# A hybrid decoder layer on one core: which engine adds the second product's weight parts, when its first finished rows are written, and how the first product's raw weights are loaded

## Chip, cores and metric

The kernel runs on one core of a Trainium2 chip. The metric is the device time of one execution in microseconds (us); lower is better. Before the change it took 2276.67 us, the median of three runs (2275.1, 2276.67 and 2277.1). Line numbers L... are those of the kernel before.

## What is computed

One decoder layer over 2048 tokens of width 1024, in float32: a block of gated linear attention and dilated attention, and behind it an MLP with a squared ReLU. The change touches the MLP alone:

```python
nm = rmsnorm(h, mlp_norm_g[l])
a = jnp.square(jax.nn.relu(jnp.einsum('bsd,df->bsf', nm, w_ff1[l])))
h = h + jnp.einsum('bsf,fd->bsd', a, w_ff2[l])
...
return rmsnorm(h, final_norm_g)
```

w_ff1 is 1024 x 4096 and w_ff2 is 4096 x 1024.

## The kernel before

**Precision.** Every float32 operand of a matmul is split in two parts: `hi`, a rounded copy made by ScalarE, and `lo`, the rest, made by VectorE (`split`, L485 to L487). A product is then three matmuls (`mm3`, L141 to L144): hi by hi, lo by hi, hi by lo. The rows "L486 ACT" and "L487 DVE" of the profile are these splits, whatever is split. In `mm3` the second matmul (L143) is the first that needs the stationary operand's `lo`.

**First product (nm by w_ff1).** It uses Winograd's form of Strassen's scheme: a 2 x 2 block product in 7 products instead of 8. The outer loop runs over 32 groups g: two halves of the tokens, and in each 16 blocks of 256 columns of w_ff1. Each group has seven products j in the order 1, 2, 6, 5, 7, 3, 4, of 12 matmuls each. The raw weights of a group (1 MB) are loaded into one of two buffers `raw1` by `load_w1` (L1282 to L1287, tile `w1raw`); `prep1` (L1289 to L1309) makes the sums of weight blocks that the scheme needs, in place (L1302, L1303, L1305, L1307, VectorE), and splits the block that product j takes into one of four buffers `w1comb`. `prep1` runs two products ahead of `product1`. When the last product's block (j = 4) is split, the buffer is free, and the load of group g + 2 is issued. `product1` takes the results out of PSUM: L1371 and L1385 on ScalarE, L1373, L1377 and L1381 on VectorE. Products 1, 6, 7 and 4 of a group add up in one PSUM bank, 5 and 3 in another; so product 4 cannot start before L1377 has read what stands after product 7. Where the second half of the tokens begins, 14 pieces of the transposed activations are loaded (tile `rb<-hTD`, L1596) and split (tile `hb`) beside the products. Sums of the results (L1335, VectorE) go to DRAM in `actD`, for the second product.

**Second product (act by w_ff2).** It has 26 phases, one for each line of the table `PRODUCTS`: a scheme of 4 x 4 by 4 x 2 blocks. A line lists which parts of w_ff2 make up the right operand and which output blocks take the result. The weights are built up step by step in a state (`state_of`, tile `bs`) of four slots, one for each quarter of a phase; a quarter is counted as n = 4 * phase + k. A part with "=" is loaded over the slot (L1497); a part with "+" or "-" is loaded into one of four buffers (`fetch_b`, L1476 to L1488, tile `rb<-w_ff`) and added or subtracted by `update_b` (L1490 to L1499). A slot can be updated for n + 4 only when the splits of n have read it. Three phases (5, 7 and 8) add two parts, sixteen add one; the first phase's updates name their own engines (V, V), which the change leaves alone. `prep_b` splits the state (tile `cb`), `prep_a` the left operand (tile `ca`, L486/L487, or L1458/L1459 where the product counts negative), both into three buffers in turn. Each n then has 24 matmuls. Within a phase the loop issues `update_b(n + 4)`, `fetch_b(n + 6)`, `prep_a(n + 2)`, `prep_b(n + 2)`, the PSUM sums of the phase before (`taken`, L1551 to L1565: L1557 on ScalarE where a block begins, L1560 on VectorE else), and the matmuls.

**Finished rows.** `done_at` holds, for each row block k of the output, the last phase that adds to it: 24, 23, 20 and 25 for k = 0 to 3. When it is taken, `output` (L1510 to L1527) normalizes four row tiles (ScalarE for the squares and the root, VectorE L1521 and L1525) and stores them. Residual rows are added into the output blocks by accumulating DMAs from GpSimd's queue (L1548).

**What sets the order.** The attention's instructions stand in a hand-written order. From the output projection on, the program is handed to a scheduler, which orders each engine's instructions by a model of their times; the Python order is its input. Each engine then runs its own list in order: an instruction that waits holds up all behind it on that engine.

Of the kernel before, what the change touches and what calls it, by code (L numbers as in the profile page):

```python
# [14 lines left out]
OP = mybir.AluOpType  # L15
# [95 lines left out]
NPH = len(PRODUCTS)  # L111
# [5 lines left out]
def emit(tc, a, stop=99):  # L117
    nc = tc.nc
    V, A, G, T, SP = nc.vector, nc.scalar, nc.gpsimd, nc.tensor, nc.sync
# [9 lines left out]
    def slot(name, dt=F32, n=SLOT):  # L129

        return up.tile([128, SLOT], dt, name=name, tag="u", bufs=25)[:, :n]

    def view(t, shape):
        n = int(np.prod(shape))
        names = "abcd"[:len(shape)]
        return t[:, :n].rearrange(f"p ({' '.join(names)}) -> p {' '.join(names)}", **dict(zip(names, shape)))
# [252 lines left out]
    def taken(n, t):  # L389

        i = t % 4
        A.activation(outputs(0)[2 * n + t // 4][:, 256 * i:256 * i + 512], held["first", n, t], AF.Copy)
        for m in (i, i + 1):
            finish(0, n, t // 4, m)
# [90 lines left out]
    def split(hi, lo, src):  # L485
        A.activation(hi, src, AF.Copy)  # L486
        V.tensor_tensor(lo, src, hi.bitcast(F32), op=OP.subtract)  # L487
# [124 lines left out]
    with tc.manual_schedule(engines={nc.tensor.engine, nc.vector.engine, nc.scalar.engine, nc.gpsimd.engine}):  # L612
# [59 lines left out]
        pv = turned(3)  # L672
        block(1, 1, 0)
        taken(0, 0)
        x_scale(4)
        first_half(3, pv)
# [9 lines left out]
        x_stat(6)  # L686
        first_half(4, pv)
        taken(1, 0)
        pv = turned(5)
        both(0, 3)  # L690
# [4 lines left out]
        both(0, 4)  # L695
        x_scale(7)
        taken(0, 2)
        first_half(6, pv)
        pv = turned(7)
# [32 lines left out]
    for at in range(7, len(jobs)):  # L732
        g = jobs[at][0]
# [542 lines left out]
    w1 = a["w_ff1"].rearrange("o (c p) n -> p (o c) n", p=128)  # L1276
# [2 lines left out]
    jobs1 = [(g, j) for g in range(2 * NP) for j in order]  # L1279
    raw1, combs1, acc1 = [], [], []  # L1280

    def load_w1(g):  # L1282
        if g < 2 * NP:
            if len(raw1) < 2:
                raw1.append(view(slot("w1raw"), (CH, 256)))
            g0 = g % NP * 256
            SP.dma_start(raw1[g % 2], w1[:, :, g0:g0 + 256])  # L1287

    def prep1(at):  # L1289

        if at >= len(jobs1):
            return
        g, j = jobs1[at]
        if not combs1:
            combs1.extend(view(c[:, 1024 * q:], (2, 4, 128)) for c in [slot("w1comb", FR) for _ in range(2)]
                          for q in range(2))
        r = raw1[g % 2]
        (a11, a12), (a21, a22) = [[r[:, 4 * k:4 * k + 4, n * 128:n * 128 + 128] for k in range(2)] for n in range(2)]
        c = combs1[at % 4]
        split(c[:, 0], c[:, 1], {1: a11, 2: a12, 6: a11, 5: a21, 7: a11, 3: a12, 4: a22}[j])  # L1300
        if j == 1:
            V.tensor_tensor(a21, a21, a22, op=OP.add)  # L1302
            V.tensor_tensor(a11, a21, a11, op=OP.subtract)  # L1303
        if j == 2:
            V.tensor_tensor(a12, a12, a11, op=OP.subtract)  # L1305
        if j == 6:
            V.tensor_tensor(a11, a22, a11, op=OP.subtract)  # L1307
        if j == 4:
            load_w1(g + 2)  # L1309

    tags = list("acdcadco")

# [87 lines left out]
    for at, t in enumerate(tiles):  # L1400
# [24 lines left out]
        if at == W1AT:  # L1425
            load_w1(0)
        if at == W1AT + 1:
            prep1(0)
            prep1(1)
# [33 lines left out]
    fetched = {}  # L1463

    def w2_part(n, k, m):

        first = 8 * (n % 4) + 2 * (k % 2) + k // 2
        return w2[:, first:first + 5:4, 512 * m:512 * m + 512]

    def state_of(n):  # L1470

        if len(state) < 2:
            state.extend(view(slot("bs"), (4, 512)) for _ in range(2))
        return state[n % 4 // 2][:, n % 2 * 2:n % 2 * 2 + 2]
# [12 lines left out]
                SP.dma_start(v, w2_part(n, k, m))  # L1487
                fetched[n].append((op, v))  # L1488

    def update_b(n, engines=(G, V)):  # L1490

        if n >= LAST:
            return
        v = state_of(n)
        for op, k, m in PRODUCTS[n // 4][2]:
            if op == "=":
                SP.dma_start(v, w2_part(n, k, m))  # L1497
        for e, (op, r) in enumerate(fetched.pop(n)):
            engines[e].tensor_tensor(v, v, r, op=OP.add if op == "+" else OP.subtract)  # L1499

    def prep_b(n):

# [7 lines left out]
    def output(C, row, i, last=False):  # L1510

        scr = fin["scr"][:, 512 * (i % 2):512 * (i % 2) + 512]
        ss, part = stat(2), stat()
        for n in range(2):
            A.activation(scr, C[n], AF.Square, accum_out=ss[:, n:n + 1])
            if n == 0:
                if last:
                    G.tensor_tensor(C[0], C[0], fin["g"][:, :512], op=OP.mult)
                A.activation(part, ss[:, 0:1], AF.Copy, bias=EPS, scale=1.0 / D)
        r = rstd_of(ss[:, 1:2], D, bias=part)  # L1520
        V.scalar_tensor_tensor(C[1], C[1], r, fin["g"][:, 512:], op0=OP.mult, op1=OP.mult)  # L1521
        if last:
            A.activation(C[0], C[0], AF.Copy, scale=r)
        else:
            V.scalar_tensor_tensor(C[0], C[0], r, fin["g"][:, :512], op0=OP.mult, op1=OP.mult)  # L1525
        SP.dma_start(out2[row:row + 128, 512:], C[1])
        (A if last else SP).dma_start(out2[row:row + 128, :512], C[0])  # L1527
# [23 lines left out]
    def taken(ph, i, p):  # L1551

        for op, k, m in PRODUCTS[ph][3]:
            if began[k, m] == ph:
                if i == 0:
                    acc2[k, m] = view(slot("sum"), (4, 512))
                A.activation(acc2[k, m][:, i], p, AF.Copy, scale=1.0 if op == "+" else -1.0)  # L1557
                continue
            v = acc2[k, m][:, i]
            V.tensor_tensor(v, v, p, op=OP.add if op == "+" else OP.subtract)  # L1560
        for k, n in done_at.items():
            if n == ph:
                half, m = divmod(i, 2)
                output([acc2[k, n][:, i] for n in range(2)], 1024 * half + 256 * k + 128 * m, i,
                       ph == NPH - 1 and i == 3)  # L1565
# [7 lines left out]
    rb.append(slot("rb"))  # L1573
    back = [*back, reload(order[3], 0), reload(order[4], 0), reload(order[5], 0, slot("rt"))]
    load_w1(1)
    for at in range(7):
        if at == 2:
            norm_to_T(*late)
        if back:
            list(back.pop(0))  # L1580
        if at == 1:
            back.append(reload(order[6], 0))
        prep1(at + 2)
        some_sums()
        product1(at)
# [12 lines left out]
    for at in range(7, len(jobs1)):  # L1598
        if at == first - 3:
            for n in range(4):  # L1600
                load_piece(n)
        prep1(at + 2)
        some_sums()
        product1(at)
        for n in parts_at.get(at, ()):
            cs = slice(1024 * (n % 2), 1024 * (n % 2) + 1024)
            split(*[v[:, cs] for v in TF[order[n // 2]]], piece(n))
            load_piece(n + 4)
        n = at + 6 - len(jobs1)
        if n == 0:  # L1610
            load_a(0)
        if 0 <= n < 4:
            fetch_b(n)
            update_b(n, (V, V))
        if n == 3:
            load_a(1)
        if n in (3, 5):
            prep_b(n // 2 - 1)
            prep_a(n // 2 - 1)
            fetch_b(n // 2 + 3)  # L1620
# [4 lines left out]
    for ph, (_, chained, _, _) in enumerate(PRODUCTS):  # L1625
        if not chained:
            held2[ph % 2] = [ps(t) for t in ("acdc", "adco")[ph % 2]]
        P = held2[ph % 2]
        for k in range(4):
            n = 4 * ph + k  # L1630
            update_b(n + 4)
            if n + 6 not in fetched:
                fetch_b(n + 6)
            prep_a(n + 2)
            prep_b(n + 2)
            if k == 1:
                begin(ph)
            if left:
                taken(ph - 1, k, left[k])
            if ph < NPH - 1 or k < 2:  # L1640
                for c in range(2):
                    for i in range(4):
                        mm2(P[i], n, c, i, not chained)
        left = P
# [60 lines left out]
```

## Time and profile before

| what | value |
|---|---|
| median of three runs | 2276.67 us |
| the profiled execution | 2279.83 us, of which the span from first to last instruction is 2278.1 us |
| granted TensorE clock, mean | 0.997 |
| first product | about 1076 to 1699 us of the span |
| second product | about 1686 to 2269.5 us of the span, overlapping the first at its start |
| behind the last matmul | 8.5 us, for the last row tile's norm and stores |

A row of the timeline gives start, duration, engine, line, operation, output<-inputs, shape and type, and in brackets how long the engine sat idle before it and what ended that. A row of the table by stage gives the stretch, its length, then busy us and number of instructions (x) of TensorE's matmuls, its weight loads, VectorE, ScalarE and GpSimd, and at the end the granted clock, the mean share of time in which the core's DMA engines were busy, and GB/s. A row of groups gives busy us and mean ns of one behind the first bar, idle time before them behind the second. A row of waits gives us in total, times and the longest. A row of DMA issues gives their number, KB each, and median us from issue to landing.

In the names of engines PE is TensorE, PEld its weight loads, DVE is VectorE, ACT is ScalarE, POOL is GpSimd and SP is SyncE (SPq: its queue of DMA issues).

### The profile page before, as it was taken

The page shows a single profiled execution, that of the slowest core. Times are in us where ns is not written, and L with a number is a line of the kernel's source. Part 1 is how long each engine was busy: PE and PEld are TensorE (multiplying, and loading weights), DVE is VectorE, ACT ScalarE, POOL GpSimd, SP SyncE. Part 2 cuts the span into 40 slices and gives each one's busy share as a digit, 9 for nine tenths or more (in the row PEclk, how much of TensorE's full clock was granted, in tenths as well). Part 3 has the DMA queues.
Part 4 walks back from the last instruction along what each step waited for, and adds up shares of the span by engine and source line. Part 5 has one row for each costly group of instructions (what it writes and reads, how often), then busy time and mean ns, then how long its engine had stood idle before and what let it go on. Part 6 is the DMA issues. An engine that isn't in the chain of part 4 may idle for free.

```text
span 2278.1 us, 35114 instructions
## 1 busy us (share of the span) xinstructions
PE 2245.7 (99%) x12508; PEld 1941.4 (85%) x12508; DVE 1627.7 (71%) x3080; ACT 1221.2 (54%) x2421; POOL 520.0 (23%) x467
## 2 busy tenths in 40 slices
PE   9999999999999999999999999999999999999998
PEld 8978998899999998888788887888888878888876
DVE  8787878766667676445777778767685567566788
ACT  6665446426877883324555557555555433333435
POOL 1210002024385673000000000000006563042452
PEclk9999999999999999999999999999999999999999
DMA  6467754776668864678645456454479988767775
GB/s 204 131 184 239 247 162 134 218 240 225 216 202 248 263 197 140 209 234 271 206 127 164 127 164 216 148 184 143 148 258 292 295 277 275 215 228 276 253 264 176
DMA packets 360927, 478.58 MB, mean 210 GB/s; under 512 B 19445, under 2 KB 268806, under 8 KB 349616
## 3 DMA queue, kind: packets, MB, share of 16 engines
q1 hardware_dynamic: 356254, 467.69, 63.8%
q0 software_dynamic: 4352, 8.39, 2.0%
q8 instruction: 98, 1.61, 0.3%
q14 instruction: 77, 0.63, 0.1%
q10 hardware_dynamic: 146, 0.27, 0.0%
HBM read 326.54 MB, written 154.44 MB: 211 GB/s over the span
## 4 chain that ended last, share of the span: by engine, by line
PE 84%; issue 4%; DVE 4%; DMA 4%; POOL 3%; ACT 1%; SPq 0%; POOLq 0%; DVEq 0%; ACTq 0%
PE ps_a L143 9%; PE ps_a L144 9%; PE ps_a L142 9%; PE ps_c L142 7%; PE ps_c L143 7%; PE ps_c L144 7%; PE ps_a L893 4%; PE ps_o L144 3%; PE ps_o L142 3%; PE ps_o L143 3%; PE ps_d L143 3%; PE ps_d L142 3%; PE ps_d L144 3%; PE ps_d L874 3%; PE ps_c L852 2%
## 5 line engine op out<-in xcount | busy, mean ns | idle before, releaser
L1499 POOL TENSOR_TENSOR bs<-bs,rb 128x1024 f32<-128x1024 f32 x72 | 219.8, 3059 | 1080.8 <-DMA actD<-ring 833.4
L486 ACT ACTIVATE cb<-bs 128x1024 fp32r<-128x1024 f32 x104 | 110.3, 1060 | 286.7 <-issue 117.3
L487 DVE TENSOR_TENSOR cb<-bs,cb 128x1024 fp32r<-128x1024 f32 x104 | 158.9, 1528 | 127.8 <-ACT cb L486 127.4
L487 DVE TENSOR_TENSOR w1comb<-w1raw,w1comb 128x512 fp32r<-128x512 f32 x224 | 153.7, 688 | 92.6 <-ACT w1comb L486 91.5
L486 ACT ACTIVATE w1comb<-w1raw 128x512 fp32r<-128x512 f32 x224 | 140.0, 628 | 79.5 <-PE ps_c L144 31.9
L893 PE MATMUL ps_a<-v,pt 128*128 128x65 f32 x1200 | 178.6, 252 | 3.7 <-ACT pt L881 2.4
L865 ACT ACTIVATE pe<-pe,O 128x256 f32<-128x256 f32 (+1 forms) x384 | 156.5, 453 | 45.9 <-DVE O L864 42.4
L893 PEld LDWEIGHTS ps_a<-v,pt 128*128 128x128 f32 x1200 | 175.2, 195 | 5.1 <-ACT pt L881 2.8
L874 PE MATMUL ps_d<-ident,pe 128*128 128x128 f32 x600 | 159.7, 279 | 0.0
L864 DVE CUSTOM_DVE_ANT_0 pe<-ps_c,nb 128x256 f32<-128x256 f32 (+1 forms) x384 | 126.4, 361 | 39.0 <-PE ps_d L874 17.8
L286 ACT ACTIVATE wcomb<-wraw 128x512 fp32r<-128x512 f32 (+2 forms) x119 | 90.0, 757 | 99.0 <-PE ps_a L143 35.0
L142 PE MATMUL ps_c<-hb,w1comb 128*128 128x512 f32 x336 | 130.9, 390 | 0.5 <-ACT xs L1371 0.5
L143 PE MATMUL ps_c<-hb,w1comb 128*128 128x512 f32 x336 | 130.7, 389 | 0.0
L144 PE MATMUL ps_c<-hb,w1comb 128*128 128x512 f32 x336 | 130.1, 389 | 0.0
L487 DVE TENSOR_TENSOR ca<-ra,ca 128x1024 fp32r<-128x1024 f32 x84 | 124.1, 1478 | 3.1 <-ACT ca L486 3.0
L144 PE MATMUL ps_c<-cb,ca 128*128 128x512 f32 x312 | 121.8, 391 | 0.0
L142 PE MATMUL ps_c<-cb,ca 128*128 128x512 f32 x312 | 121.7, 390 | 0.0
L143 PE MATMUL ps_c<-cb,ca 128*128 128x512 f32 x312 | 121.6, 390 | 0.0
L351 POOL TENSOR_TENSOR acc<-acc,misc 128x264 f32<-128x264 f32 (+1 forms) x32 | 38.6, 1220 | 314.0 <-DMA wraw<-w_in 201.4
L874 PEld LDWEIGHTS ps_d<-ident,pe 128*128 128x128 f32 x600 | 110.2, 188 | 0.1
L1362 ACT ACTIVATE acc<-acc 128x512 f32<-128x512 f32 x96 | 60.6, 632 | 76.7 <-DVE acc L1381 48.4
L142 PE MATMUL ps_a<-wo,mT 128*128 128x512 f32 x256 | 101.4, 396 | 0.0
(411 smaller groups left out, 7103.2 us busy)
## 6 DMA issues: line engine op xcount, KB each, us to landing
ra<-actD SPq DMA_DIRECT2D x52, 1024.0 KB, 7.7
actD<-ring SPq DMA_DIRECT2D x176, 256.0 KB, 2.2
rb<-w_ff SPq DMA_DIRECT2D x88, 512.0 KB, 6.0
bs<-w_ff SPq DMA_DIRECT2D x72, 512.0 KB, 5.7
w1raw<-w_ff SPq DMA_DIRECT2D x32, 1024.0 KB, 6.2
k<-kD SPq DMA_DIRECT2D x16, 1024.0 KB, 7.9
wraw<-w_in SPq DMA_DIRECT2D x48, 256.0 KB, 3.8
cmb<-boD SPq DMA_DIRECT2D x16, 528.0 KB, 7.7
```

What stands on the lines that cost most here:

```text
L142: T.matmul(out, sh, mh, start=first, stop=False, **kw)
L143: T.matmul(out, sl, mh, start=False, stop=False, **kw)
L144: T.matmul(out, sh, ml, start=False, stop=last, **kw)
L286: A.activation(hi, src, AF.Copy, scale=sc)
L486: A.activation(hi, src, AF.Copy)
L487: V.tensor_tensor(lo, src, hi.bitcast(F32), op=OP.subtract)
L864: V.tensor_tensor_reduce(p, s, bias, scale=1.0, scalar=BIG, op0=OP.add, op1=OP.min, accum_out=nm)
L865: A.activation(p, p, AF.Exp, bias=nm, scale=-1.0)
L874: T.transpose(pb[:, i * 128:i * 128 + 128], src, ident)
L893: T.matmul(self.b.opsum[:, n % 4], self.pt[:, i * 128:i * 128 + 128], self.b.v[:, blk, cols], start=first, stop=last)
L1362: A.activation(v, v, AF.Relu)
L1499: engines[e].tensor_tensor(v, v, r, op=OP.add if op == "+" else OP.subtract)
```

## The change

Three edits.

A. `update_b` of the second product: where two parts are added, both are added by VectorE, one behind the other; where one is added, GpSimd adds it, as before. Before, the first went to GpSimd and the second to VectorE.

B. A row block of the output that is complete is written one phase later, but for those that end in the last three phases. With the table's `done_at` that moves row block 2 from phase 20 to phase 21 (its work is issued with the phase after each).

C. `load_w1` loads in two halves of 512 KB. Half 0 (blocks a11 and a21) of group g + 2 is issued after the split for product 7, half 1 (a12 and a22) after that for product 4. The sums that stood with product 1 now stand with product 2, ahead of the one that stood there.

```diff
-    def load_w1(g):
+    def load_w1(g, halves=(0, 1)):
         if g < 2 * NP:
             if len(raw1) < 2:
                 raw1.append(view(slot("w1raw"), (CH, 256)))
             g0 = g % NP * 256
-            SP.dma_start(raw1[g % 2], w1[:, :, g0:g0 + 256])
+            for k in halves:
+                SP.dma_start(raw1[g % 2][:, 4 * k:4 * k + 4], w1[:, 4 * k:4 * k + 4, g0:g0 + 256])
...
-        if j == 1:
+        if j == 2:
             V.tensor_tensor(a21, a21, a22, op=OP.add)
             V.tensor_tensor(a11, a21, a11, op=OP.subtract)
-        if j == 2:
             V.tensor_tensor(a12, a12, a11, op=OP.subtract)
         if j == 6:
             V.tensor_tensor(a11, a22, a11, op=OP.subtract)
-        if j == 4:
-            load_w1(g + 2)
+        if j in (7, 4):
+            load_w1(g + 2, (0,) if j == 7 else (1,))
...
-    def update_b(n, engines=(G, V)):
+    def update_b(n, engines=None):
...
-        for e, (op, r) in enumerate(fetched.pop(n)):
-            engines[e].tensor_tensor(v, v, r, op=OP.add if op == "+" else OP.subtract)
+        sums = fetched.pop(n)
+        for e, (op, r) in enumerate(sums):
+            (engines or ((G,), (V, V))[len(sums) - 1])[e].tensor_tensor(v, v, r, op=OP.add if op == "+" else OP.subtract)
...
-            if n == ph:
+            if ph == (n if n > NPH - 4 else n + 1):
                 half, m = divmod(i, 2)
                 output([acc2[k, n][:, i] for n in range(2)], 1024 * half + 256 * k + 128 * m, i,
                        ph == NPH - 1 and i == 3)
```

## The prediction, made before the changed kernel ran

> **What bounds the kernel now.** I read the page's busy times first, then the list of who waited for whom on TensorE, then a table of busy time by stage.
>
> ```profile
> span 2278.1 us, 35114 instructions
> PE 2245.7 (99%) x12508; PEld 1941.4 (85%) x12508; DVE 1627.7 (71%) x3080; ACT 1221.2 (54%) x2421; POOL 520.0 (23%) x467
> ```
> ```profile
> PE ps_a L143 <- DVE ca L487: 4.5, 3, 2.8
> ...
> PE ps_d L143 <- DVE w1comb L487: 1.8, 2, 1.4
> ...
> PE ps_a L143 <- DVE ca L1459: 0.9, 2, 0.7
> ```
> ```profile
> 1085.00:1115.00 30.00, 27.53 (x121) 21.88 (x120) 22.76 (x37) 17.94 (x31) 0.00 (x0) 1.00 0.70 212
> 1115.00:1370.00 255.00, 255.00 (x1127) 211.15 (x1126) 188.94 (x380) 142.22 (x243) 0.00 (x0) 1.00 0.47 147
> 1370.00:1405.00 35.00, 32.57 (x139) 25.40 (x138) 32.69 (x53) 26.05 (x40) 0.00 (x0) 1.00 0.70 227
> 1405.00:1685.00 280.00, 280.00 (x1237) 231.86 (x1236) 210.89 (x423) 158.86 (x271) 0.00 (x0) 1.00 0.54 171
> ...
> 1829.00:1879.00 50.00, 47.24 (x199) 36.52 (x198) 36.56 (x36) 17.05 (x17) 30.81 (x11) 1.00 0.87 281
> 1879.00:2150.00 271.00, 271.00 (x1197) 224.38 (x1197) 184.77 (x156) 100.23 (x100) 77.87 (x30) 1.00 0.74 249
> 2150.00:2190.00 40.00, 37.21 (x158) 30.32 (x157) 38.50 (x33) 20.50 (x42) 22.91 (x9) 0.96 0.80 269
> ```
>
> TensorE is the bound: 2245.7 of 2278.1 us. Only what makes it wait can be won, so the change is worth what it does to a few waits. Matmuls overlap, so idle time understates a stall; I count matmuls instead. Undisturbed, one starts every 280.00/1237 = 0.2264 us (1405 to 1685; 1879 to 2150 gives the same). A stretch's loss is its length less its count times 0.2264: 2.6 us from 1085 to 1115 (first product's start), 3.5 from 1370 to 1405 (its change of halves), 4.9 from 1829 to 1879 (second product, phases 6 to 8), 4.2 from 2150 to 2190 (its first finished rows). That makes 15.2 us, the most that the touched stages can give. The long rows between them lose nothing.
>
> **Part A, the weight sums.** One group (n) of the second product in the bad stretch, VectorE first, then GpSimd:
>
> ```profile
> 1838.97 1.23 DVE L1499 TENSOR_TENSOR bs<-bs,rb 128x1024 f32<-128x1024 f32 x1 [2.29 <-POOL bs L1499]
> 1840.11 1.22 DVE L487 TENSOR_TENSOR cb<-bs,cb 128x1024 fp32r<-128x1024 f32 x1
> 1841.24 1.22 DVE L1459 SCALAR_TENSOR_TENSOR ca<-ra,ca 128x1024 fp32r<-128x1024 f32 x1
> 1844.75 1.23 DVE L1499 TENSOR_TENSOR bs<-bs,rb 128x1024 f32<-128x1024 f32 x1 [2.29 <-POOL bs L1499]
> ...
> 1869.48 1.23 DVE L1499 TENSOR_TENSOR bs<-bs,rb 128x1024 f32<-128x1024 f32 x1 [3.28 <-DMA rb<-w_ff]
> ```
> ```profile
> 1841.41 3.31 POOL L1499 TENSOR_TENSOR bs<-bs,rb 128x1024 f32<-128x1024 f32 x1 [2.47 <-DVE cb L487]
> ```
> ```profile
> L1560 DVE TENSOR_TENSOR sum<-sum,ps_c 128x512 f32<-128x512 f32 x4 | 2.7, 678 | 0.0
> ```
>
> It is a ring: cb's split (L487) frees the state, GpSimd adds the first part (3.31 us), VectorE adds the second, and only then may VectorE, whose queue is in order, split the next cb and ca. VectorE idles 2.29 us in it. One turn takes 1844.75 - 1838.97 = 5.78 us, but TensorE needs a group every 24 x 0.2264 = 5.43. So it stalls a little in group after group.
>
> The change takes 12 GpSimd sums away (three phases with two sums, four groups each: 12 x 3.31 = 39.7 us of GpSimd) and adds 12 sums to VectorE, at the 1.14 us at which such rows follow each other: 13.7 us. A turn becomes four VectorE instructions, 4 x 1.14 = 4.56 us, and a phase with one set of four PSUM sums (0.68 each) 4 x 4.56 + 2.7 = 20.9 us against TensorE's 21.7. VectorE fits, barely, and the ring is gone. Queued behind the added sums are the same splits as now. On GpSimd the residual loads (L1548) that stood behind the removed sums go out sooner, into a stretch whose DMA share is 0.87, which adds to the risk that weight loads land late. The new last wait is the second part's load, which must land before the second sum, as the last row (3.28 us for a load) shows once. Most of the lateness of phases 6 to 8 goes, and I leave 0.6 us for one load that comes late: 4.3 us won. Bounds: 4.9 (all) and nothing (loads take over).
>
> **Part B, finished rows a phase later.**
>
> ```profile
> 2170.75 0.74 DVE L1525 SCALAR_TENSOR_TENSOR sum<-sum,stats,gf 128x512 f32<-128x512 f32 x1
> 2171.41 2.90 DVE L1521 SCALAR_TENSOR_TENSOR sum<-sum,stats,gf 128x512 f32<-128x512 f32 x1
> 2174.23 2.88 DVE L1525 SCALAR_TENSOR_TENSOR sum<-sum,stats,gf 128x512 f32<-128x512 f32 x1
> ...
> 2179.49 1.21 DVE L487 TENSOR_TENSOR ca<-ra,ca 128x1024 fp32r<-128x1024 f32 x1
> ```
> ```profile
> 2180.76 0.50 PE L143 MATMUL ps_a<-cb,ca 128*128 128x512 f32 x1 [2.79 <-DVE ca L487]
> ...
> 2182.60 0.63 PE L143 MATMUL ps_d<-cb,ca 128*128 128x512 f32 x1
> 2183.03 0.63 PE L144 MATMUL ps_d<-cb,ca 128*128 128x512 f32 x1
> ```
>
> This stall is made by the eight L1521/L1525 of row block 2, which stand ahead of a ca split that TensorE needs. The edit asks for them a phase later. But the program's text is only the scheduler's input. In the changed program as built, everything behind the last of the edited sums stands in the same order with the same waits: VectorE's last 264, ScalarE's last 222, SyncE's last 163, TensorE's last 2474. The scheduler put the rows back where they were. The stretch before, 1879 to 2150, is undisturbed, so the stall is met in the same state: gain 0. Bounds: 0, and 4.2 if timing upstream shifted it away. After the wait, matmuls start 0.43 us apart (2182.60 to 2183.03) instead of 0.23; that part of the loss is in the 4.2. [...]
>
> **Part C, raw weights in halves.** VectorE, SyncE and TensorE at the first stall, and around one undisturbed group:
>
> ```profile
> 1102.31 0.69 DVE L1302 TENSOR_TENSOR w1raw<-w1raw 128x512 f32<-128x512 f32 x1 [3.67 <-DMA w1raw<-w_ff]
> 1102.92 0.68 DVE L1307 TENSOR_TENSOR w1raw<-w1raw 128x512 f32<-128x512 f32 x1
> 1103.52 0.69 DVE L487 TENSOR_TENSOR w1comb<-w1raw,w1comb 128x512 fp32r<-128x512 f32 x1
> ```
> ```profile
> 1092.59 0.81 SPq L1287 DMA_DIRECT2D w1raw<-w_ff  x1
> ...
> 1147.81 0.37 SPq L1287 DMA_DIRECT2D w1raw<-w_ff  x1
> ```
> ```profile
> 1104.26 0.50 PE L143 MATMUL ps_d<-hb,w1comb 128*128 128x512 f32 x1 [1.45 <-DVE w1comb L487]
> ...
> 1153.90 0.39 PE L142 MATMUL ps_a<-hb,w1comb 128*128 128x512 f32 x1
> ```
> ```profile
> 1150.53 0.69 DVE L1303 TENSOR_TENSOR w1raw<-w1raw 128x512 f32<-128x512 f32 x1
> 1151.38 0.69 DVE L1377 TENSOR_TENSOR acc<-ps_c,acc 128x512 f32<-128x512 f32 x1 [0.15 <-PE ps_c L144]
> 1152.04 0.69 DVE L487 TENSOR_TENSOR w1comb<-w1raw,w1comb 128x512 fp32r<-128x512 f32 x1
> 1153.42 0.69 DVE L1302 TENSOR_TENSOR w1raw<-w1raw 128x512 f32<-128x512 f32 x1 [0.68 <-DMA w1raw<-w_ff]
> ```
> ```profile
> actD<-ring SPq DMA_DIRECT2D x176, 256.0 KB, 2.2
> rb<-w_ff SPq DMA_DIRECT2D x88, 512.0 KB, 6.0
> ```
> ```profile
> 1390.15 1.06 ACT L486 ACTIVATE hb<-rb 128x1024 fp32r<-128x1024 f32 x1 [1.16 <-DMA rb<-hTD]
> ```
>
> It adds 32 SyncE issues (0.37 us each, 11.8 us spread over 600 us of a queue that is not on the path) and moves no byte. Three effects.
>
> First stall: L1302 (group 2) waits until 1102.31 for a load issued at 1092.59, and the w1comb split that TensorE needs stands behind it. The order there is unchanged. With the first half issued two products earlier (2 x 12 x 0.2264 = 5.4 us), the second has 512 KB less to move, 1.9 us at the table's 281 GB/s, and lands up to that much sooner. The stall is 1.45 us idle, some 1.7 with the restart (its first matmul takes 0.50); I take 1.3 us as won. Bounds: 0 and 1.7.
>
> Steady groups, a risk: in the built program the scheduler, now counting on a shorter load, sets L1302 ahead of L1303, L1377 and the next w1comb split. The group's last product (j = 4, from 1153.90) accumulates on the bank that L1377 reads, and L1377 now stands behind a wait for a load. From the issue at 1147.81 that leaves 1153.90 - 1147.81 - 0.61 x 2 - 0.69 - 0.05 = 4.1 us for the half to land (VectorE instructions of this size start 0.61 apart). The whole load took 5.6 (1147.81 to 1153.42). A half has no row; 2.2 us for 256 KB and 5.6 for 1 MB give 3.3 on a line, which I take because the queue is idle there; the upper bound is 6.0, the median of the 512 KB loads in a busy stage. At 3.3 nothing is lost, and I charge 0.2 us in all (bounds 0 and the slower rival below). [...]
>
> Change of halves: ScalarE waits for hTD pieces (1.16 us at 1390.15), which queue behind a whole w1raw load. With half of it sent earlier those pieces land sooner, but the built order puts one more hb split ahead of a w1comb split that is late already. I take 0.3 us won; bounds 2.0 won, 1.5 lost.
>
> **Sum.** 4.3 + 0 + 1.3 - 0.2 + 0.3 = 5.7 us. The profiled execution took 2279.83 us (1.7 around the span), 3.2 above the runs' median of 2276.67. So 2274.1 on its scale and 2271.0 on the median's.
>
> **Rivals.**
> Loads take over. The stretch from 1829 to 1879 already moves 281 GB/s at a DMA share of 0.87; the same bytes in 45 us would be 312. Against it: 0.87 leaves room, and each load now goes out earlier, since its buffer is freed earlier. Part A would then give 1.5 us of its 4.3: 2273.8.
> First product stalls (slower). The half lands later than 4.1 us, L1377 is late, and TensorE waits in each of 14 groups (every other one). At a landing of 4.8 it is 0.7 + 0.1 for the restart, times 14 = 11.2 us lost: 2271.0 - 0.2 + 11.2 = 2282.0. It decides from 4.1 + 5.9/14 = 4.5 us on. For it: 6.0 for loads of this size elsewhere; against it: DMA share 0.47 in this stage.
> The late rows do work, or the 2180 stall dissolves: 4.2 more, 2266.8. Against it: the equal order.
>
> **How the numbers follow.** Forecast 0.60 (own range 2268 to 2274), loads 0.18, first product 0.16, late rows 0.06. 0.2%, about what a measurement of this kernel can tell from no change, is 4.6 us: faster means below 2272.1. The forecast's range lies above that in about a sixth of cases (0.10). Faster: 0.50 + 0.06, and 0.01 of the loads case, 0.57; same 0.10 + 0.17 = 0.27; slower 0.16. The range takes in the late rows below (2266.5) and reaches into the first-product case above (2278.5).
>
> **What would show it.** Right: no TensorE wait on ca between 1829 and 1879, and that stretch's successor holding some 220 matmuls per 50 us; GpSimd 60 sums and VectorE 28; the wait of about 2.8 us on ca in phase 22 still there; L1302's wait for w1raw well below its 0.7 to 3.7 us. Wrong: short TensorE waits in every other group of the first product, or VectorE's second sums waiting for rb.

## The result and the profile after

| kernel | median, us | runs | ratio, 95% interval |
|---|---|---|---|
| before | 2275.55 (2271.38 to 2278.33) | 22 | |
| changed | 2271.51 (2265.31 to 2274.87) | 22 | 0.9982 [0.9975, 0.9988] |

The change makes the kernel 4.0 us faster; the forecast was 5.7 us. From here on line numbers are those of the kernel whose trace is shown: in the changed one, L1302, L1303 and L1499 have become L1303, L1304 and L1500, L1521/L1525 are L1522/L1526, and the load L1287 is L1288.

The page of the changed kernel, its span, its busy times and its group of GpSimd's sums:

```profile
span 2269.7 us, 35245 instructions
...
PE 2242.1 (99%) x12508; PEld 1941.8 (86%) x12508; DVE 1632.6 (72%) x3092; ACT 1219.0 (54%) x2421; POOL 481.5 (21%) x455
...
L1500 POOL TENSOR_TENSOR bs<-bs,rb 128x1024 f32<-128x1024 f32 x60 | 179.1, 2993 | 1069.9 <-DVE ca L487 836.2
```

GpSimd has 60 sums, and VectorE 12 instructions more than before (3092 to 3080). Its table by stage (stretch, length, busy us and number on TensorE, weight loads, VectorE, ScalarE, GpSimd, then clock, DMA share, GB/s):

```profile
1085.00:1115.00 30.00, 28.62 (x124) 22.84 (x123) 23.65 (x39) 17.28 (x31) 0.00 (x0) 1.00 0.67 210
1370.00:1405.00 35.00, 31.04 (x133) 24.44 (x133) 30.94 (x48) 25.38 (x40) 0.00 (x0) 1.00 0.72 243
...
1685.00:1829.00 144.00, 142.26 (x628) 117.48 (x627) 104.88 (x98) 70.92 (x90) 61.37 (x26) 1.00 0.94 296
1829.00:1879.00 50.00, 50.00 (x222) 41.44 (x221) 45.94 (x43) 18.70 (x19) 16.13 (x8) 1.00 0.98 309
...
2150.00:2190.00 40.00, 37.87 (x168) 31.04 (x167) 40.00 (x33) 20.50 (x42) 24.31 (x8) 1.00 0.82 287
```

With the prediction's measure (length less count x 0.2264), 1829 to 1879 loses nothing now (199 matmuls before, 222 after, at the same 50 us). The first stall is a little smaller (121 to 124), the change of halves larger (139 to 133). 1685 to 1829, which lost nothing before (637 x 0.2264 = 144.2), now loses 144 - 628 x 0.2264 = 1.8 us. Its row before:

```profile
1685.00:1829.00 144.00, 144.00 (x637) 119.22 (x636) 88.92 (x86) 72.23 (x92) 74.83 (x31) 1.00 0.93 289
```

TensorE's waits in the whole trace of the changed kernel show where:

```profile
PE ps_a L143 <- DVE ca L487: 3.9, 2, 2.1
...
PE ps_d L143 <- DVE w1comb L487: 1.7, 2, 0.9
```

One of the two waits for ca is the old one in phase 22 (2.1 us). The other, 1.7 us, is new and stands where the first product passes into the second.

The two traces differ by more than the medians do: 8.4 us of span. Code that the change doesn't touch starts the first product at 1076.1 us before and at 1073.3 after. So one trace can't size a term, and the table below has every trace of the study. Its losses are counted between fixed matmuls, so that a stretch holds the same work in every kernel (us from its first to its last start, less count x 0.2264): the first product's first 140; its 1180th to 1400th, where the halves change; the 60 on either side of the second product's first; the second product's 500th to 1000th (phases 5 to 10); and its 1960th to 2340th (phases 20 to 24). The first product's matmuls are counted here with eight short transposes (L510) near its start. They lower the column of the first stall by about 1 us in every kernel alike, so only differences of it mean something. The column of the change of halves leaves out a last wait of 0.7 to 1.3 us that stands just behind its stretch in every kernel.

| kernel | first product starts | first stall | change of halves | passage | phases 5 to 10 | phases 20 to 24 |
|---|---|---|---|---|---|---|
| before | 1076.1 | 2.4 | 2.9 | 0.0 | 5.3 | 4.8 |
| changed | 1073.3 | 1.3 | 4.5 | 2.1 | 0.1 | 2.5 |
| a_only | 1071.4 | 2.0 | 2.7 | 0.0 | 0.1 | 3.1 |
| c_only | 1072.7 | -0.2 | 4.3 | 0.9 | 4.4 | 3.0 |
| b_only | 1072.1 | 1.2 | 3.7 | 0.0 | 5.3 | 4.8 |
| a_b_keep | 1073.9 | 4.3 | 3.2 | 0.0 | 0.1 | 2.4 |
| a_split | 1074.6 | 1.7 | 3.1 | 0.0 | 0.1 | 1.3 |
| best | 1073.6 | 0.6 | 2.4 | 0.0 | 0.1 | 2.1 |
| v_all | 1073.3 | 1.7 | 3.5 | 0.0 | 0.9 | 4.9 |
| h_half2 | 1074.5 | 1.8 | 4.6 | 0.0 | 4.2 | 6.6 |
| vg | 1072.3 | 4.4 | 4.2 | 0.0 | 0.1 | 5.7 |
| split_halves | 1074.0 | -0.1 | 4.7 | 1.3 | 0.1 | 1.3 |

Between the named stretches only v_all loses more than 2 us (8.8 us, phases 10 to 20).

### The profile page after: what moved, and what is told of

Read it like the earlier page. It is cut to its first block, busy times and chain, and to the rows that moved or that the text cites. A ratio compares the mean times of both kernels' runs of the same rounds, so it can differ in the third digit from the quotient of the medians.

```text
span 2269.7 us, 35245 instructions
## 1 busy us (share of the span) xinstructions
PE 2242.1 (99%) x12508; PEld 1941.8 (86%) x12508; DVE 1632.6 (72%) x3092; ACT 1219.0 (54%) x2421; POOL 481.5 (21%) x455
## 4 chain that ended last, share of the span: by engine, by line
PE 90%; DMA 3%; DVE 2%; issue 2%; POOL 1%; ACT 1%; POOLq 0%; SPq 0%; DVEq 0%; ACTq 0%
PE ps_a L143 10%; PE ps_a L142 10%; PE ps_a L144 10%; PE ps_c L143 8%; PE ps_c L142 8%; PE ps_c L144 8%; PE ps_a L893 4%; PE ps_d L143 4%; PE ps_o L144 4%; PE ps_d L144 4%; PE ps_o L143 4%; PE ps_o L142 4%; PE ps_d L142 4%; PE ps_d L874 3%; PE ps_c L852 2%; PE ps_c L854 2%
## 5 line engine op out<-in xcount | busy, mean ns | idle before, releaser
L1500 POOL TENSOR_TENSOR bs<-bs,rb 128x1024 f32<-128x1024 f32 x60 | 179.1, 2993 | 1069.9 <-DVE ca L487 836.2
```

The costliest lines, as they stand in the source:

```text
L1500: (engines or ((G,), (V, V))[len(sums) - 1])[e].tensor_tensor(v, v, r, op=OP.add if op == "+" else OP.subtract)
```

## The experiments

### The sums alone (a_only)

```diff
-    def update_b(n, engines=(G, V)):
+    def update_b(n, engines=None):
...
-        for e, (op, r) in enumerate(fetched.pop(n)):
-            engines[e].tensor_tensor(v, v, r, op=OP.add if op == "+" else OP.subtract)
+        sums = fetched.pop(n)
+        for e, (op, r) in enumerate(sums):
+            (engines or ((G,), (V, V))[len(sums) - 1])[e].tensor_tensor(v, v, r, op=OP.add if op == "+" else OP.subtract)
```

> Only the weight sums are changed (second sums on VectorE); first product and finished rows as before. As built, TensorE, ScalarE and SyncE have the order of before, so anything that moves is the sums. Theory 1 (the ring was the whole stall): the stretch from 1829 to 1879 holds some 220 matmuls instead of 199, 4.9 us are won, ratio 0.9978 (2270.7 us beside 2275.6). Theory 2 (loads take over, as the prediction's first rival had it): 1.5 us, ratio 0.9993. Theory 3 (the shorter wait in phase 22 that the changed kernel's profile shows, 2.5 instead of 3.2 us with no slow matmuls behind it, comes from the sums too): 4.9 + 2.4 = 7.3 us, ratio 0.9968.

Measured: 2270.49 us against 2275.82, ratio 0.9974 [0.9964, 0.9983]. Its table by stage:

```profile
1829.00:1879.00 50.00, 50.00 (x223) 41.40 (x222) 47.58 (x40) 18.42 (x19) 17.15 (x8) 1.00 0.96 294
...
2150.00:2190.00 40.00, 37.30 (x165) 30.54 (x164) 40.00 (x27) 18.44 (x35) 26.57 (x9) 1.00 0.80 275
```

Phases 5 to 10 lose 0.1 instead of 5.3 us. DMA share and rate rise as the loads' rival had it (0.96, 294 GB/s), and VectorE's second sums wait four times for a part's load (6.0 us in all, 2.4 at the longest) without any loss to TensorE: that rival falls. Phases 20 to 24 lose 3.1 instead of 4.8, but that is no gain of the sums: c_only, with the old sums, has 3.0 there. The ratio alone can't part theory 1 from theory 3; this row does. The sums alone are not distinguishable from the whole change, so the other two edits together bring nothing that shows.

### The halves alone (c_only)

```diff
-            SP.dma_start(raw1[g % 2], w1[:, :, g0:g0 + 256])
+            for k in halves:
+                SP.dma_start(raw1[g % 2][:, 4 * k:4 * k + 4], w1[:, 4 * k:4 * k + 4, g0:g0 + 256])
...
-        if j == 4:
-            load_w1(g + 2)
+        if j in (7, 4):
+            load_w1(g + 2, (0,) if j == 7 else (1,))
```

(with the sums of j = 1 moved to j = 2 as in the change; h_half2 below leaves them in place, and from just behind the change of halves on it has the same order as this kernel)

> Only the raw weights in halves; weight sums and finished rows as before. Theory 1 (the halves cost more than they win: first stall 0.5 us better, change of halves 1.5 us worse, a new wait for ca of 2.0 us at the passage to the second product): 3.0 us slower, ratio 1.0013, and these three waits stand in this profile without the sums. Theory 2 (the prediction's terms: 1.3 - 0.2 + 0.3): 1.4 us faster, ratio 0.9994. Theory 3 (the new wait at the passage belongs to the sums, so it is absent here): 1.0 us slower, ratio 1.0004.

Measured: 2275.43 us against 2275.82, ratio 0.9997 [0.9988, 1.0006]: no difference that shows. The stages do differ, and cancel: first stall gone, change of halves 4.3, passage 0.9. Theory 3 falls, since the wait at the passage is there with the old sums. Theories 1 and 2 had the signs of some terms each; theory 1's sum, a ratio of 1.0013, lies outside the interval, and theory 2's 0.9994 inside. The passage in this trace (SyncE's issue, VectorE, TensorE):

```profile
1662.23 0.92 SPq L1497 DMA_DIRECT2D bs<-w_ff  x2
...
1664.86 0.69 DVE L1377 TENSOR_TENSOR acc<-ps_d,acc 128x512 f32<-128x512 f32 x1 [0.15 <-PE ps_d L144]
...
1668.21 1.22 DVE L1499 TENSOR_TENSOR bs<-bs,rb 128x1024 f32<-128x1024 f32 x1 [2.66 <-DMA bs<-w_ff]
...
1685.37 0.50 PE L143 MATMUL ps_a<-cb,ca 128*128 128x512 f32 x1 [0.61 <-DVE ca L487]
```

and in the kernel with the sums alone, which has whole loads:

```profile
1660.96 1.09 SPq L1497 DMA_DIRECT2D bs<-w_ff  x2
...
1664.35 0.68 DVE L1377 TENSOR_TENSOR acc<-ps_d,acc 128x512 f32<-128x512 f32 x1
...
1666.35 1.23 DVE L1500 TENSOR_TENSOR bs<-bs,rb 128x1024 f32<-128x1024 f32 x1 [1.31 <-DMA bs<-w_ff]
```

The halves changed the scheduler's order far beyond the loads. One more store of the first product's sums (`actD<-ring`, 256 KB) now stands ahead of the first two bs loads of the second product: they go out 2.6 us ahead of L1377 instead of 3.4. VectorE waits for them in its queue (2.66 us instead of 1.31), and the ca split that TensorE needs stands further back in that queue.

### The rows' edit alone (b_only)

```diff
-            if n == ph:
+            if ph == (n if n > NPH - 4 else n + 1):
```

> Only the finished rows a phase later in the program's text. As built, every engine has the same instructions in the same order as before. Theory: the same program, ratio 1.000 within 0.1%, the wait for ca in phase 22 as before; what differs between the two profiles is then what one execution differs from another. Rival (something that the order doesn't show, a semaphore or an address, differs): a ratio outside 0.999 to 1.001.

Measured: 2275.48 us against 2275.82, ratio 0.9996 [0.9987, 1.0005]. The edit alone is the kernel before, as built and in time: in the two traces every engine's instructions stand in the same order. So this trace is a second one of the same program: between the two, the first product's start differs by 4.0 us, the first stall by 1.3, the change of halves by 0.7, and phases 5 to 10 and 20 to 24 by less than 0.1. The wait in phase 22, in GpSimd's, VectorE's and TensorE's rows:

```profile
2166.20 0.74 DVE L1525 SCALAR_TENSOR_TENSOR sum<-sum,stats,gf 128x512 f32<-128x512 f32 x1
2166.82 2.40 POOL L1499 TENSOR_TENSOR bs<-bs,rb 128x1024 f32<-128x1024 f32 x1 [5.87 <-DMA bs<-w_ff]
2166.87 2.90 DVE L1521 SCALAR_TENSOR_TENSOR sum<-sum,stats,gf 128x512 f32<-128x512 f32 x1
2169.51 2.51 POOL L1499 TENSOR_TENSOR bs<-bs,rb 128x1024 f32<-128x1024 f32 x1 [0.30 <-DMA bs<-w_ff]
2169.69 2.88 DVE L1525 SCALAR_TENSOR_TENSOR sum<-sum,stats,gf 128x512 f32<-128x512 f32 x1
...
2176.22 0.63 PE L143 MATMUL ps_a<-cb,ca 128*128 128x512 f32 x1 [2.77 <-DVE ca L487]
```

Two of the eight scalings take 2.9 us instead of 0.74, and each begins within 0.2 us behind the start of a GpSimd sum. Those 2 x 2.16 us are more than the wait of 2.77. Each of the two ends 0.55 us behind the end of its sum (2169.77 behind 2169.22, 2172.57 behind 2172.02): 2.90 - 0.74 = 2.16 us is about the rest of a sum of 2.40.

### The rows really a phase later (a_b_keep)

The sums alone, the rows' edit, and two lines that hold it:

```diff
+        keep = (lambda x: x) if last else tc.keep_in_program_order
-        V.scalar_tensor_tensor(C[1], C[1], r, fin["g"][:, 512:], op0=OP.mult, op1=OP.mult)
+        keep(V.scalar_tensor_tensor(C[1], C[1], r, fin["g"][:, 512:], op0=OP.mult, op1=OP.mult))
...
-            V.scalar_tensor_tensor(C[0], C[0], r, fin["g"][:, :512], op0=OP.mult, op1=OP.mult)
+            keep(V.scalar_tensor_tensor(C[0], C[0], r, fin["g"][:, :512], op0=OP.mult, op1=OP.mult))
```

> Sums on VectorE, and the finished rows a phase later with VectorE's two scalings of each held to the program's order, so that as built the eight scalings of row block 2 stand behind four more pairs of cb and ca splits. First product as before. Theory 1 (those eight scalings make the wait in phase 22): that wait goes, and 2150 to 2190 holds some 176 matmuls instead of 158; 4 us beyond the sums alone, ratio 0.9960. Theory 2 (the wait is only moved: the rows' buffers or the late splits of the next phase are late instead): a wait of 1 us or more within 15 us behind it, and no more than 1.5 us beyond the sums alone, ratio 0.9971 or above. Theory 3 (what follows was hidden by the wait): slower than the sums alone.

Measured: 2271.14 us, ratio 0.9974 [0.9964, 0.9984], the same as with the sums alone. Theory 2 holds. VectorE and TensorE in this trace:

```profile
2173.04 2.29 DVE L1523 SCALAR_TENSOR_TENSOR sum<-sum,stats,gf 128x512 f32<-128x512 f32 x1
2175.25 2.88 DVE L1527 SCALAR_TENSOR_TENSOR sum<-sum,stats,gf 128x512 f32<-128x512 f32 x1
...
2184.96 1.21 DVE L487 TENSOR_TENSOR ca<-ra,ca 128x1024 fp32r<-128x1024 f32 x1
...
2186.23 0.50 PE L143 MATMUL ps_a<-cb,ca 128*128 128x512 f32 x1 [1.99 <-DVE ca L487]
```

The eight scalings now stand ahead of the next phase's splits. The heap has moved, two of its scalings (2.29 and 2.88 us) again fall beside GpSimd's sums, and TensorE waits 2.0 us at the other place. What the edit says it does, done really, is worth nothing that shows.

### Half of the rows a phase later (a_split)

Against a_b_keep:

```diff
-            if ph == (n if n > NPH - 4 else n + 1):
+            if ph == (n if n > NPH - 4 or i < 2 else n + 1):
...
-        keep = (lambda x: x) if last else tc.keep_in_program_order
+        keep = (lambda x: x) if last or i < 2 else tc.keep_in_program_order
```

> Sums on VectorE, and of each early row block only the last two of its four row tiles a phase later, held to the program's order; first product as before. As built, VectorE has four scalings, two pairs of splits, and then the other four scalings, instead of eight scalings close together. Theory 1 (the wait in phase 22 is the number of scalings in one heap ahead of a ca split): with half a heap before each of the two splits neither wait is left above 0.5 us, 2.5 to 3.1 us beyond the sums alone, ratio 0.9962. Theory 2 (VectorE is full there, so that any order is late somewhere): a wait of 1.5 us or more remains between 2150 and 2200, ratio 0.9970 or above.

Measured: 2266.1 us against 2275.72, ratio 0.9961 [0.9947, 0.9975]. Phases 20 to 24 lose 1.3 us, with one wait left:

```profile
PE ps_a L143 <- DVE ca L487: 0.8, 1, 0.8
```

The wait is above theory 1's 0.5 us and below theory 2's 1.5. The ratio is theory 1's, but its interval takes in theory 2's 0.9970 and overlaps that of the sums alone, so the row shows the gain and the time doesn't settle it. In this trace three of the four scalings ahead of the late split still take 2.3 to 2.9 us beside GpSimd's sums (2171.67, 2175.08, 2177.29), against two of eight in a_b_keep, and the wait is 0.8 us instead of 2.0. So it isn't the slowed scalings alone: the smaller heap goes with the smaller wait.

### The same with halves for two loads (best)

Against the changed kernel, with a_split's rows and the sums of j = 1 back in their place:

```diff
+        whole = g >= 2
+        if j == 4 and whole:
+            load_w1(g + 2)
+        elif j in (7, 4) and not whole:
+            load_w1(g + 2, (0,) if j == 7 else (1,))
```

> As the kernel with half of the rows a phase later, and besides halves for the third and fourth load of raw weights alone (the first two that take the place of others); all other loads whole, and as built the order of TensorE, ScalarE, VectorE and GpSimd is that of the kernel without halves. Theory 1 (the halves win at the first stall, and what they lose comes from the changed order further on): the first stall falls from 1.2 to 2.5 us to 1.3 us or less, change of halves and passage to the second product stay as without halves, 1 us beyond the kernel with the rows alone, ratio 0.9957. Theory 2 (the halves win nothing, the first stall varies by itself): the same ratio as that kernel.

Measured: 2266.84 us against 2275.72, ratio 0.9967 [0.9955, 0.998]. The first stall is 0.6 us, and change of halves and passage are as with whole loads (2.4 and 0.0), as theory 1 had it; the gain of about 1 us doesn't show in the time. With a_split it is the fastest of all, 9 to 10 us under before, and the two can't be told apart.

### All sums on VectorE (v_all)

Against the sums alone:

```diff
-            (engines or ((G,), (V, V))[len(sums) - 1])[e].tensor_tensor(v, v, r, op=OP.add if op == "+" else OP.subtract)
+            (engines or (V, V))[e].tensor_tensor(v, v, r, op=OP.add if op == "+" else OP.subtract)
```

> All weight sums on VectorE, GpSimd has none (finished rows and first product as before). Theory 1 (VectorE's scalings and splits of 2.3 to 3.4 us in phase 22, instead of 0.7 to 1.2, are those beside a GpSimd sum): without GpSimd's sums they all take 0.7 or 1.2 us, and the wait in phase 22 is below 1 us; the single sums' phases then need 4 x 1.14 us less cover than before, and nothing else is late: ratio 0.9960. Theory 2 (VectorE, with 12 + 60 more sums of 1.14 us, is the bound in the phases with rows or accumulations): waits for ca in several phases, slower than the kernel with the double sums alone, ratio 0.9980 or above.

Measured: 2281.71 us, ratio 1.0031 [1.002, 1.0043]: slower, by 0.3%. Rows of the timeline from phase 22:

```profile
2173.22 0.75 DVE L1522 SCALAR_TENSOR_TENSOR sum<-sum,stats,gf 128x512 f32<-128x512 f32 x1
...
2176.81 0.75 DVE L1522 SCALAR_TENSOR_TENSOR sum<-sum,stats,gf 128x512 f32<-128x512 f32 x1
```

and VectorE's waits from 1885 to 2180 us:

```profile
DVE bs L1500 <- DMA bs<-w_ff: 71.5, 20, 7.2
```

Theory 1 holds for the scalings: with no GpSimd sum, all eight take 0.75 us. The rest of it falls (TensorE still waits 1.8 us in phase 22, at 2173.36, ahead of the heap, and 8.8 us are lost in phases 10 to 20), but not for theory 2's reason, since VectorE isn't full: it idles 71.5 us in its queue, 20 times, up to 7.2 us, for bs loads, with splits behind the waiting sum. In the kernel with the sums alone VectorE has no such wait there and GpSimd waits for these loads instead (in the changed kernel, with the same sums, 162.6 us in 20 waits from 1885 to 2180), and phases 10 to 20 lose 0.3 us.

### Halves in the second half alone (h_half2)

```diff
+        whole = g + 2 < NP
+        if j == 4 and whole:
+            load_w1(g + 2)
+        elif j in (7, 4) and not whole:
+            load_w1(g + 2, (0,) if j == 7 else (1,))
```

> Halves for the loads of the first product's second half alone; everything else as before. Theory 1 (the wait at the passage to the second product comes from halves near it, which set one more store of the sums ahead of the first two bs loads): the wait for ca at the passage is there, 0.9 to 2.1 us, while first stall (1.2 to 2.5 us) and change of halves (2.7 to 3.7 us) are as with whole loads. Theory 2 (it comes from lateness that the change of halves hands on): no wait at the passage. The time itself, within 0.1% of before, decides nothing.

Measured: 2277.85 us against 2275.72, ratio 1.0009 [0.9999, 1.0019]. No wait at the passage, and yet neither theory is right, since the order there is that of the halves everywhere. Issue, L1384 (L1377 of before) and the first sum in this trace:

```profile
1666.45 0.93 SPq L1504 DMA_DIRECT2D bs<-w_ff  x2
...
1669.07 0.69 DVE L1384 TENSOR_TENSOR acc<-ps_d,acc 128x512 f32<-128x512 f32 x1 [0.15 <-PE ps_d L144]
...
1671.50 1.23 DVE L1506 TENSOR_TENSOR bs<-bs,rb 128x1024 f32<-128x1024 f32 x1 [1.74 <-DMA bs<-w_ff]
```

and in the changed kernel, with the wait that follows:

```profile
1664.44 0.92 SPq L1497 DMA_DIRECT2D bs<-w_ff  x2
...
1667.06 0.69 DVE L1377 TENSOR_TENSOR acc<-ps_d,acc 128x512 f32<-128x512 f32 x1 [0.15 <-PE ps_d L144]
...
1671.17 1.23 DVE L1500 TENSOR_TENSOR bs<-bs,rb 128x1024 f32<-128x1024 f32 x1 [3.41 <-DMA bs<-w_ff]
...
1688.71 0.50 PE L143 MATMUL ps_a<-cb,ca 128*128 128x512 f32 x1 [1.74 <-DVE ca L487]
```

The issue stands 2.6 us ahead of L1377 in both. From issue to the sum it is 5.0 us here, 6.0 in c_only and 6.7 in the changed kernel, and the passage loses 0.0, 0.9 and 2.1. So the order took the slack away, and each execution's load then decides. The 6.6 us in phases 20 to 24 come with a wait of 3.6 us for ScalarE's ca split, which most other traces don't have. GpSimd and ScalarE in this trace:

```profile
2169.95 8.64 POOL L1506 TENSOR_TENSOR bs<-bs,rb 128x1024 f32<-128x1024 f32 x1 [6.81 <-DMA bs<-w_ff]
...
2189.63 1.06 ACT L486 ACTIVATE ca<-ra 128x1024 fp32r<-128x1024 f32 x1 [9.94 <-DMA ra<-actD]
```

It is b_only's meeting of scalings and sums the other way round. Here the GpSimd sum begins 0.2 us behind a scaling (2169.73), all eight scalings take 0.74 us, and the sum takes 8.64 instead of 2.4. It holds the buffer that SyncE's next part load needs, SyncE waits 11.4 us for it, and the left operand's load (L1453) stands behind that in its queue. Which of the two begins first differs between traces in which both engines have the same instructions in the same order there (b_only and h_half2).

### The two sums swapped (vg)

Against the sums alone:

```diff
-            (engines or ((G,), (V, V))[len(sums) - 1])[e].tensor_tensor(v, v, r, op=OP.add if op == "+" else OP.subtract)
+            (engines or ((G,), (V, G))[len(sums) - 1])[e].tensor_tensor(v, v, r, op=OP.add if op == "+" else OP.subtract)
```

> The kernel before with the two sums of a group swapped: VectorE adds the first part, GpSimd the second; GpSimd keeps its 72 sums, VectorE its 16, and as built VectorE's order differs in two places by four instructions. Theory 1 (the loss of phases 6 to 8 was VectorE's wait, in its queue, for GpSimd's sum): VectorE's sum now waits for no GpSimd sum, GpSimd's is not needed before a cb split four groups later, and 1829 to 1879 loses 0.1 us, as with both sums on VectorE: ratio 0.9976. Theory 2 (GpSimd's 3.3 us each were the loss, wherever they stand): the cb splits wait for GpSimd instead, 4 to 5 us are lost there as before, ratio 0.9997.

Measured: 2273.13 us against 2276.97, ratio 0.998 [0.9971, 0.999]. Stage, and rows of VectorE and GpSimd:

```profile
1829.00:1879.00 50.00, 50.00 (x222) 41.41 (x221) 50.00 (x37) 19.29 (x19) 33.98 (x14) 1.00 0.91 300
```

```profile
1838.83 1.21 DVE L1500 TENSOR_TENSOR bs<-bs,rb 128x1024 f32<-128x1024 f32 x1
...
1841.10 3.42 DVE L487 TENSOR_TENSOR ca<-ra,ca 128x1024 fp32r<-128x1024 f32 x1
```
```profile
1840.12 3.32 POOL L1500 TENSOR_TENSOR bs<-bs,rb 128x1024 f32<-128x1024 f32 x1 [2.30 <-DVE bs L1500]
```

Theory 1 holds: GpSimd does as many sums as before, they last 3.3 us as before, and phases 5 to 10 lose 0.1 us. The loss was VectorE's wait in its queue for the other engine's sum. Beside a GpSimd sum a ca split takes 3.42 us, and VectorE is full (50.00 of 50 us); both sums on VectorE leave it 4 us in 50 (45.94). Its ratio stands 0.0006 above a_only's, inside both intervals; this trace also loses 4.4 us at the first stall, with slow matmuls, and 5.7 in phases 20 to 24, where the same wait for ScalarE's ca split stands as in h_half2 (a GpSimd sum of 7.79 us at 2167.45, and SyncE 11.5 us behind it).

### The whole change with half of the rows later (split_halves)

a_split's edit on top of the changed kernel.

> The whole change, with half of each early block's rows really a phase later (two scalings' heaps instead of one). Theory 1 (the halves add nothing to the time: first stall won, change of halves and passage lost): the ratio of the same kernel without halves, 0.9961 to 0.9967, and a passage wait of 0 to 2.1 us that follows the landing of the first bs load (5.0 us: 0, 6.0: 1.0, 6.7: 2.1). Theory 2 (the halves cost 1 us by run and run): ratio 0.9968 or above.

Measured: 2268.63 us against 2276.97, ratio 0.9963 [0.9951, 0.9976], and the passage:

```profile
1663.61 0.93 SPq L1497 DMA_DIRECT2D bs<-w_ff  x2
...
1670.14 1.22 DVE L1500 TENSOR_TENSOR bs<-bs,rb 128x1024 f32<-128x1024 f32 x1 [3.22 <-DMA bs<-w_ff]
```

6.5 us from issue to sum, and 1.3 us lost: between c_only and the changed kernel, as theory 1 had it. The ratio is theory 1's; its interval takes in theory 2's 0.9968 too. The halves neither add nor cost anything that shows in the time.

## Why the prediction was right, point by point

- **Part A** carried the forecast and was right in cause and nearly in size: 4.3 us forecast, 5.2 measured (5.3 to 0.1 in phases 5 to 10). The 0.6 us kept back for a late load weren't needed, though the stage runs at a DMA share of 0.98. A second sum on VectorE does wait for its part, which the prediction had as a sign of being wrong (four times in a_only); it costs TensorE nothing. That the ring was a wait in VectorE's queue is shown by vg: the wait taken out, with GpSimd's sums kept, wins the same.
- **Part B, nothing**, was right: alone it is the same program. The 2.3 us by which phases 20 to 24 differ between the two traces are not its work: c_only, without it, has 3.0 there. Of the 4.8 us before, some 1.6 are eight matmuls that start 0.43 us apart instead of 0.23 (8 x (0.43 - 0.23)), where the granted clock was 0.50 (2182.0 to 2185.2). "Made by the eight L1521/L1525 of row block 2" was the right place, but left out half of the cause: two of them take 2.9 us because a GpSimd sum runs. The quoted rows of before already had them (2171.41 and 2174.23), 0.1 and 0.2 us behind GpSimd sums that begin at 2171.31 and 2174.07.
- **Part C, the first stall**: 1.3 us forecast. Over all traces whole loads lose 1.2 to 4.4 us there (eight traces, mean 2.4; 1.8 without the two that have slow matmuls and a granted clock of 0.94 from 1085 to 1115, a_b_keep and vg), halves -0.2 to 1.3 (four traces, mean 0.4): 1.4 to 2.0 won. The 281 GB/s in its working are the row of phases 6 to 8; the row of this stall has 212, which makes 2.5 us of the 1.9. The bound of 1.7 held the term down either way.
- **Part C, steady groups**: 0.2 us forecast, nothing lost from 1115 to 1370. The half, issued at 1143.87, was there at 1147.57, after 3.7 us, where 3.3 were expected and 4.1 were free:

```profile
1143.87 0.37 SPq L1288 DMA_DIRECT2D w1raw<-w_ff  x1
...
1147.57 0.69 DVE L1303 TENSOR_TENSOR w1raw<-w1raw 128x512 f32<-128x512 f32 x1 [1.00 <-DMA w1raw<-w_ff]
1148.18 0.68 DVE L1304 TENSOR_TENSOR w1raw<-w1raw 128x512 f32<-128x512 f32 x1
1148.78 0.68 DVE L1377 TENSOR_TENSOR acc<-ps_c,acc 128x512 f32<-128x512 f32 x1
```

  The landing was underestimated, and the rival that the first product stalls falls by little: 0.4 us in this group, and less than 0.1 in the closest of the steady groups (issued at 1220.03, there at 1224.08). Its wait for L1377 shows once, just behind the change of halves: 0.1 us in this trace and 0.2 in c_only. That no more was lost is partly luck. One sign failed: the wait of L1302 (L1303) for its load is hardly shorter, 37.4 us in 29 waits against 44.2 in 31 before, since the built order also asks for the half earlier.
- **Part C, change of halves**: 0.3 us won was forecast, 1.3 are lost (whole 2.4 to 4.2, mean 3.2; halves 4.3 to 4.7, mean 4.5), inside the bound of 1.5. The step that failed: "with half of it sent earlier those pieces land sooner". ScalarE's waits for these pieces are hardly shorter: 3.1 to 4.0 us per trace with whole loads (mean 3.5), 2.4 to 3.6 with halves (mean 3.2). So what the prediction set against them, one more hb split ahead of a late w1comb split, was left as a cost. VectorE and TensorE in c_only:

```profile
1385.43 2.35 DVE L487 TENSOR_TENSOR hb<-rb,hb 128x1024 fp32r<-128x1024 f32 x2
...
1391.52 0.50 PE L143 MATMUL ps_d<-hb,w1comb 128*128 128x512 f32 x1 [0.82 <-DVE w1comb L487]
```

  Two hb splits stand together there, where the kernel before has one. This wait for w1comb is 0.8 to 1.4 us in the four traces with halves (mean 1.1) and 0 to 1.1 in the eight others (mean 0.3), which is 0.8 of the 1.3. With the wait that the column leaves out, the means are 4.3 and 5.4, and 1.1 are lost.
- **The passage** had no term. The prediction compared the two orders behind the last edited sum, and stage by stage where the kernel before waited; at the passage it waited nowhere, so a changed order there was not priced. It costs 0 to 2.1 us, mean 1.1 over four traces.
- **The sum**: 5.2 + 0 + 2.0 - 1.3 - 1.1 = 4.8 from the means, 4.0 measured with an interval of 2.7 to 5.7 (0.0012 and 0.0025 of 2275.55). Part C, forecast at 1.4 us won, is about nothing. So the sum came out near because A was 0.9 us too small and C 1.8 too large, and the time forecast, 2271.0, lies within 0.5 us of the measured one also because before itself measured 1.1 us less than the 2276.67 it started from. That nearness is luck; the mechanism of A is not. By the prediction's own measure for "faster", 0.2%, the 4.0 us are just short, though the interval is clear of no change.

## What to carry to other kernels

Where two engines add to the same tile in turn, ask which of them stands in an ordered queue with urgent work behind the wait: swapping the two sums won as much as taking one engine out (phases 5 to 10 lose 0.1 us in vg and in a_only, 5.3 before). The reverse holds for loads: a step that waits for a late load belongs on the engine with nothing urgent behind it, here GpSimd (phases 10 to 20 lose 0.3 us in a_only, 8.8 in v_all), as long as the buffer that it holds isn't what another queue waits for (in h_half2 SyncE waits 11.4 us for it, and TensorE 3.6 us for the ca split behind that). When a scheduler orders the program, compare the built order of every stage, also of those that wait for nothing yet; and moving a heap of work by a whole phase only moved its wait here (2.0 us in a_b_keep), while halving it shrank the wait (0.8 in a_split).

## What the hardware showed that was not expected

- **VectorE behind a GpSimd sum, and the reverse.** 0.74 us become 2.9 (b_only) and 1.21 become 3.42 (vg), where a GpSimd sum began first; without GpSimd's sums all eight scalings take 0.75 (v_all). Where a GpSimd sum began behind a scaling with a chain of scalings and splits to follow, it took 8.64 us (h_half2). GpSimd's own sum takes 2.4 us where it began first (b_only, at 2166.82) and 3.3 beside VectorE's chain of splits (before, at 1841.41).
- **The clock after short waits.** TensorE waits 2.20 us in a_b_keep's first stall, and 1.4 us after it starts again its matmuls come 0.43 us apart (granted clock 0.94 from 1085 to 1115, where before has 1.00):

```profile
1102.34 0.50 PE L143 MATMUL ps_d<-hb,w1comb 128*128 128x512 f32 x1 [2.20 <-DVE w1comb L487]
...
1103.72 0.63 PE L142 MATMUL ps_d<-hb,w1comb 128*128 128x512 f32 x1
1104.15 0.63 PE L143 MATMUL ps_d<-hb,w1comb 128*128 128x512 f32 x1
```

  After the longer wait of a_only in phase 22, 2.70 us, no such stretch follows (granted clock 1.00 from 2150 to 2190):

```profile
2170.12 0.50 PE L143 MATMUL ps_a<-cb,ca 128*128 128x512 f32 x1 [2.70 <-DVE ca L487]
2170.46 0.40 PE L144 MATMUL ps_a<-cb,ca 128*128 128x512 f32 x1
```

  The length of the wait alone doesn't decide.
